# Head norms of an attention: the reciprocal root as exp(-ln/2) on ScalarE in place of a VectorE reciprocal and a ScalarE root

## The chip, the cores and the metric

The kernel runs as one program on one core of a Trainium2 chip. A core has five engines that run side by side, each through its own list of instructions in order: TensorE (PE, matrix products, with its weight loads shown as PEld), VectorE (DVE), ScalarE (ACT), GpSimd (POOL) and SyncE (SP, which here only issues DMAs). They wait for each other by semaphores. The metric is the time of one execution on the device, in microseconds (us). The kernel before took 3070.99 us in the median of three runs (3069.37 to 3074.17).

## What is computed

Two layers with a mixer and a feed-forward part each; the second layer's mixer is an attention with 16 heads of 64 numbers, whose queries and keys are normed per head before the scores:

```
def rms_norm(x, g):
    xf = x.astype(jnp.float32)
    y = xf * lax.rsqrt(jnp.mean(xf * xf, axis=-1, keepdims=True) + NORM_EPS)
    return (y * g.astype(jnp.float32)).astype(x.dtype)

def fox_mixer(h, in_w, f_b, q_norm_g, k_norm_g, out_w):
...
    q, k, v, f_logit, og = jnp.split(h @ in_w, [D, 2 * D, 3 * D, 3 * D + H], axis=-1)
    q = rms_norm(q.reshape(B, S, H, E), q_norm_g)
    k = rms_norm(k.reshape(B, S, H, E), k_norm_g)
...
        s = jnp.einsum('bhqe,bkhe->bhqk', qb, k).astype(jnp.float32) * scale
        s = s + cq[..., None] - cum[:, :, None, :]
        s = jnp.where(qpos[:, None] >= key_pos[None, :], s, -jnp.inf)
        p = jax.nn.softmax(s, axis=-1)
        return jnp.einsum('bhqk,bkhe->bqhe', p.astype(v.dtype), v)
```

The sequence has S = 512 tokens, the width is D = 1024, E = 64. The change concerns `lax.rsqrt(mean + NORM_EPS)` in the two head norms, and nothing else.

## The kernel before

The program runs the first layer (a gated recurrence, then a feed-forward part that picks experts), then the attention, then the second layer's feed-forward part. Matrix products keep single precision by splitting each operand into a high and a low part (`hi`, `lo`) and adding three products; the splits cost ScalarE a copy and VectorE a subtraction each (`split`, L252 and L253; for weights, L180 and L182).

The attention is `fox`. The heads are worked off in eight pairs, since two heads of 64 fill the 128 partitions. For each pair j:

- `prepare(j)` calls `heads_norm`. It projects the queries and the keys of the pair (`proj_t`, 24 matmuls each, L496 to L498, tile pacc of which there are two). ScalarE squares each projection (sq, L1348) and copies it with its gain (raw, L1350). Matmuls with a matrix of ones sum the squares over each head into one tile of 128x256 in PSUM (ssq, L1352), where the sums for queries and keys of both heads and both halves of the tokens stand in eight of its rows. Then comes the reciprocal root of that tile: VectorE scales and adds the epsilon (L1355) and takes the reciprocal (L1356), ScalarE takes the root (L1357). The tile is split (rh on ScalarE, rl on VectorE), spread over the partitions by matmuls (rsb, L1366 and L1367) and multiplied into raw (L1368). After this, ScalarE and VectorE make the operands qs, qx, ks, kx of the scores (L1395 to L1408).
- `attend(j)` takes the two heads in turn, and in each four blocks of 128 queries: scores (s, L1426 and L1427), mask (L1428), row maximum (nm, L1430), exponential (p, L1433, on ScalarE), its reciprocal sum and scaling (L1434, L1435, on VectorE), transposes on TensorE (tp, L1438), a split of these (pth and ptl, L252 and L253), and the products with the values (o, L1443 to L1445).

Pairs 0 and 1 are prepared first; after that pair j + 2 is prepared behind the attention of pair j, and behind the last two pairs the gates of the output (`gate`) are projected instead. So TensorE always has projection matmuls that depend on little beside the weights, and they stand between the matmuls of the attention, which wait for ScalarE and VectorE.

The order on each engine isn't that of the code: a scheduler lays it out when the program is built, by its own estimates of how long each instruction takes, except for instructions that are pinned to the order of the code (`keep_in_program_order`). From then on it is fixed. ScalarE needs a table of coefficients for its functions; the program's builder puts a load of another table (ACT_TABLE_LOAD) ahead of an instruction whose function isn't in the table that is loaded. [...]

Beside the attention, a few rows of the next stage's modulation are computed on VectorE (`during`, L215), and SP and POOL fetch weights.

Of the kernel before, what the change touches and what calls it, by code (L numbers as in the profile page):

```python
# [4 lines left out]
F32 = mybir.dt.float32  # L5
# [5 lines left out]
AF = mybir.ActivationFunctionType  # L11
OP = mybir.AluOpType
# [9 lines left out]
EPS = 1e-6  # L22
FH = 16
FE = 64
# [226 lines left out]
def split(g, hi, lo, raw, eng=None):  # L251
    g.nc.scalar.activation(hi, raw, AF.Copy)  # L252
    (eng or g.nc.vector).tensor_sub(lo, raw, hi)  # L253
# [235 lines left out]
def proj_t(g, psum, h, n=S, bank=None):  # L489

    nc = g.nc
    whi, wlo = g.stream.take()
    hhi, hlo = h
    ps = (psum.tile([128, S], F32, name="pacc", tag="acc") if bank is None else bank)[:, :n]
    for k in range(KD):
        nc.tensor.matmul(ps, whi[:, k, :], hhi[:, k, :n], start=(k == 0), stop=False)  # L496
        nc.tensor.matmul(ps, whi[:, k, :], hlo[:, k, :n], start=False, stop=False)  # L497
        nc.tensor.matmul(ps, wlo[:, k, :], hhi[:, k, :n], start=False, stop=(k == KD - 1))  # L498
    return ps
# [748 lines left out]
def fox(g, norm_fn, fb, qg, kg, during, grow_fn, after):  # L1248

    tc, nc = g.tc, g.nc  # L1250
    V, A, T = nc.vector, nc.scalar, nc.tensor
    cx = g.dram.tile([FH, 2, 4, S], F32R, name="cx")
    with pool(tc, name="foxy", bufs=1) as fy:
# [4 lines left out]
        with pool(tc, name="fox", bufs=1) as fp:  # L1258
# [28 lines left out]
            kgc = fp.tile([128, 1], F32, name="kgc")  # L1287
            nc.sync.dma_start(kgc, kg)
            V.tensor_scalar(qgc, qgc, FE ** -0.5, None, op0=OP.mult)
            fbc = fp.tile([FH, 1], F32, name="fbc")  # L1290
            nc.sync.dma_start(fbc, fb)
            sel = fp.tile([128, 128 + NU * 4 - 2], F32, name="sel")
# [5 lines left out]
            def chosen(i, u):  # L1298

                r = NU * 4 - 2 - u * 4 - i * 2  # L1300
                return sel[:, r:r + 128]
# [35 lines left out]
            with pool(tc, name="foxw", bufs=2) as fw, \  # L1337
                    pool(tc, name="fps", bufs=2, space=PSUM) as psum:

                def heads_norm(parts):  # L1340

                    n = S // NU
                    ss = psum.tile([128, n], F32, name="ssq", tag="n", bufs=1)
                    raw = []
                    for i, gc in enumerate(parts):
                        ps = proj_t(g, psum, h)
                        sq = fw.tile([128, S], F32, name="sq", tag="sq", bufs=1)
                        A.activation(sq, ps, AF.Square)  # L1348
                        r = fw.tile([128, S], F32, name="raw", tag=f"raw{i}")
                        A.activation(r, ps, AF.Copy, scale=gc)  # L1350
                        for u in range(NU):
                            T.matmul(ss, chosen(i, u), sq[:, u * n:(u + 1) * n], start=(i == 0 and u == 0),  # L1352
                                     stop=(i == 1 and u == NU - 1))
                        raw.append(r)
                    V.tensor_scalar(ss, ss, 1.0 / FE, EPS, op0=OP.mult, op1=OP.add)  # L1355
                    V.reciprocal(ss, ss)  # L1356
                    A.activation(ss, ss, AF.Sqrt)  # L1357
                    rh = fw.tile([128, n], F32R, name="rh", tag="rh", bufs=1)
                    rl = fw.tile([128, n], F32R, name="rl", tag="rl", bufs=1)
                    split(g, rh, rl, ss)  # L1360
                    out = []
                    for i, r in enumerate(raw):
                        b = psum.tile([128, S], F32, name="rsb", tag="n", bufs=1)
                        for u in range(NU):
                            us = slice(u * n, (u + 1) * n)
                            T.matmul(b[:, us], selT[:, i, u, :], rh, start=True, stop=False)  # L1366
                            T.matmul(b[:, us], selT[:, i, u, :], rl, start=False, stop=True)  # L1367
                        V.tensor_mul(r, r, b)  # L1368
                        out.append(r)
                    return out  # L1370
# [15 lines left out]
                def prepare(j):  # L1386
                    qn, kn = heads_norm((qgc, kgc))
                    stacks = []
                    for par in range(2):
                        own = slice(par * 64, par * 64 + 64)  # L1390
                        oth = slice(64 - par * 64, 128 - par * 64)
                        hd = j * 2 + par
                        qs = fw.tile([128, S], F32R, name="qs", tag="qs", bufs=4)
                        qx = fw.tile([68, S], F32R, name="qx", tag="qx", bufs=4)
                        A.activation(qs[own], qn[own], AF.Copy)  # L1395
                        V.tensor_sub(qs[oth], qn[own], qs[own])
                        A.activation(qx[0:64], qn[own], AF.Copy)
                        nc.gpsimd.dma_start(qx[64:68], cx[hd, 0])
                        stacks.append([qs, qx])
                    for par in range(2):  # L1400
                        own = slice(par * 64, par * 64 + 64)
                        oth = slice(64 - par * 64, 128 - par * 64)
                        hd = j * 2 + par
                        ks = fw.tile([128, S], F32R, name="ks", tag="ks", bufs=4)
                        kx = fw.tile([68, S], F32R, name="kx", tag="kx", bufs=4)
                        A.activation(ks[own], kn[own], AF.Copy)
                        A.activation(ks[oth], kn[own], AF.Copy)
                        V.tensor_sub(kx[0:64], kn[own], ks[own])  # L1408
                        nc.gpsimd.dma_start(kx[64:68], cx[hd, 1])
                        stacks[par] += [ks, kx]  # L1410
                    return stacks
# [58 lines left out]
def model(tc, *aps):  # L1470
# [4 lines left out]
    with ExitStack() as ctx:  # L1475
# [35 lines left out]
        def flat(n):  # L1511
# [7 lines left out]
             lambda p: mod("l0_ffn", p, gate, 4, ring=8), lambda p: mod("l1_mix", p, bufs=4, ring=8),  # L1519
             lambda p: mod("l1_ffn", p, first[:M1], 4, ring=8), 3, PUMPS[0])  # L1520
        fox(g, normed("l1_mix"), *arg("fox_", "fb", "qg", "kg"), lambda p: (mod("l1_ffn", p, first[M1:], 1),),
            grow("l1_mix"), lambda p: ())
        peer(g, normed("l1_ffn"), flat("l1_u"), flat("l1_v"), grow("l1_ffn"),
# [98 lines left out]
```

## Time and profile before

| what | us |
|---|---|
| median of three runs | 3070.99 |
| lowest, highest run | 3069.37, 3074.17 |
| the profiled execution | 3075.46 |
| span in its trace | 3073.7 |
| the stretch in which heads are normed and attended, from 1569 to 1789 us | 220 |

The profiled execution is one of its own, with its own time; the span is the part of it from the first to the last instruction, 1.8 us shorter. Times in the trace are counted from the start of the span. By stages the engines were busy as follows (one row for each stretch; busy us of each engine with the number of instructions, then the granted TensorE clock, the share of the DMA engines and GB/s):

```profile
520.00:1420.00 900.00, 894.90 (x4981) 803.93 (x4980) 788.94 (x1020) 399.09 (x544) 401.11 (x296) 1.00 0.95 360
1420.00:1569.00 149.00, 145.80 (x678) 122.03 (x676) 107.11 (x177) 62.73 (x102) 15.16 (x29) 1.00 0.48 169
1569.00:1789.00 220.00, 214.93 (x1107) 172.84 (x1106) 189.50 (x457) 175.32 (x365) 18.05 (x35) 1.00 0.21 71
1900.00:3073.00 1173.00, 1161.38 (x6429) 1050.54 (x6427) 980.61 (x1877) 513.25 (x690) 429.61 (x326) 1.00 0.81 297
```

The first number behind the stretch is its length, then PE, PEld, DVE, ACT, POOL. A line of a group reads: line of the code, engine, operation, output and inputs by the program's names, shapes, how often, busy time and mean duration in ns, and the idle time of that engine just before it with what ended that. A line of the waits reads: who waited for whom, us in total, times, longest. PEld waits are those of the weight loads, which run ahead of the matmuls.

### The profile page before, as it was taken

What the parts mean: (1) busy time and instruction counts of PE and PEld (TensorE: products, weight loads), DVE (VectorE), ACT (ScalarE), POOL (GpSimd) and SP (SyncE); (2) the same over time, 40 slices, a digit from 0 to 9 for tenths busy, and PEclk for the clock granted to TensorE, in tenths of its full rate; (3) what the DMA queues carried; (4) which work ended last, traced back from release to release, by engine and by line L of the source; (5) the groups of instructions that cost most, each with busy time, mean ns of one, the idle gap of its engine ahead of it and who ended that gap; (6) DMA issues with size and microseconds to landing.
All of it is one profiled execution on the core that took longest, in us unless ns stands there. A gap on an engine that the chain in (4) does not pass through costs nothing.

```text
span 3073.7 us, 44567 instructions
## 1 busy us (share of the span) xinstructions
PE 3021.1 (98%) x16196; PEld 2672.5 (87%) x16196; DVE 2567.1 (84%) x5272; ACT 1479.7 (48%) x2184; POOL 972.2 (32%) x842
## 2 busy tenths in 40 slices
PE   7999999999999999999999999999999999999999
PEld 5778899998888888888777778899998888888888
DVE  7866989878889888898679868799968888888787
ACT  6764247873333333333468843367853333333332
POOL 0001430006665145563011003400035544445451
PEclk9999999999999999999999999999999999999999
DMA  7543345779999999998332123346799999999995
GB/s 286 177 159 129 103 148 207 263 292 394 393 375 396 351 356 382 384 370 316 123 114 85 63 110 127 120 167 242 271 350 377 349 357 349 355 344 359 346 339 189
DMA packets 295470, 815.85 MB, mean 265 GB/s; under 512 B 24625, under 2 KB 147537, under 8 KB 266705
## 3 DMA queue, kind: packets, MB, share of 16 engines
q1 hardware_dynamic: 164304, 388.77, 35.3%
q0 software_dynamic: 89408, 321.43, 27.7%
q10 hardware_dynamic: 41536, 102.80, 8.7%
q8 instruction: 127, 2.08, 0.3%
q14 instruction: 95, 0.77, 0.1%
HBM read 731.89 MB, written 81.02 MB: 264 GB/s over the span
## 4 chain that ended last, share of the span: by engine, by line
PE 75%; DVE 13%; issue 5%; ACT 3%; DMA 3%; POOL 0%; DVEq 0%; SPq 0%; POOLq 0%; ACTq 0%
PE vacc L1159 31%; PE pacc L496 11%; PE pacc L498 11%; PE pacc L497 11%; PE gps L1002 3%; DMA at<-ascr 2%; DVE wlo L182 2%; DVE accg L1072 1%; PE oacc L539 1%; PE oacc L540 1%; PE oacc L538 1%; DVE ge L909 1%; DVE tk L834 1%; DVE idxs L833 1%; DVE idxs L836 1%
## 5 line engine op out<-in xcount | busy, mean ns | idle before, releaser
L180 ACT ACTIVATE whi<-wraw 128x1024 fp32r<-128x1024 f32 (+1 forms) x646 | 663.6, 1033 | 579.4 <-PE pacc L497 338.2
L496 PE MATMUL pacc<-hhi,whi 128*128 128x384 f32 (+1 forms) x2600 | 915.3, 352 | 0.0
L498 PE MATMUL pacc<-hhi,wlo 128*128 128x384 f32 (+1 forms) x2600 | 908.7, 350 | 6.1 <-DVE wlo L182 5.8
L497 PE MATMUL pacc<-hlo,whi 128*128 128x384 f32 (+1 forms) x2600 | 906.7, 349 | 0.0
L182 DVE TENSOR_TENSOR wlo<-wraw,whi 128x1024 fp32r<-128x1024 f32 (+2 forms) x580 | 699.2, 1210 | 184.5 <-ACT whi L180 183.3
L1159 PE MATMUL vacc<-whi,wl 128*128 128x512 f32 x1536 | 600.2, 391 | 0.0
L1159 PE MATMUL vacc<-wlo,wh 128*128 128x512 f32 x1536 | 599.9, 391 | 0.0
L1159 PE MATMUL vacc<-whi,wh 128*128 128x512 f32 x1536 | 597.6, 389 | 0.0
L498 PEld LDWEIGHTS pacc<-hhi,wlo 128*128 128x128 f32 x2600 | 488.7, 188 | 32.7 <-DVE wlo L182 9.8
L497 PEld LDWEIGHTS pacc<-hlo,whi 128*128 128x128 f32 x2600 | 489.2, 188 | 26.9
L496 PEld LDWEIGHTS pacc<-hhi,whi 128*128 128x128 f32 x2600 | 489.2, 188 | 26.4
L1149 ACT ACTIVATE wh<-at 128x384 fp32r<-128x384 f32 x256 | 133.9, 525 | 737.3 <-DVE at L1145 456.3
L1042 POOL DMA_INDIRECT rows<-in_l_u_dram,ei x256 | 383.3, 1497 | 280.5 <-DVE rows L1055 221.7
L1042 POOL DMA_INDIRECT rows<-in_l_v_dram,ei x256 | 369.0, 1441 | 322.0 <-DVE accg L1072 281.6
L1159 PEld LDWEIGHTS vacc<-whi,wl 128*128 128x128 f32 x1536 | 288.2, 188 | 60.3
L1159 PEld LDWEIGHTS vacc<-wlo,wh 128*128 128x128 f32 x1536 | 288.2, 188 | 57.5
L1159 PEld LDWEIGHTS vacc<-whi,wh 128*128 128x128 f32 x1536 | 288.4, 188 | 57.1
L1072 DVE SCALAR_TENSOR_TENSOR accg<-rows,act,accg 128x1024 f32<-128x1024 f32 x254 | 324.5, 1278 | 0.4
L1055 DVE SCALAR_TENSOR_TENSOR rows<-rows,hn 128x1024 f32<-128x1024 f32 x256 | 304.0, 1218 | 0.0
L1145 DVE TENSOR_TENSOR at<-at,gtile 128x384 f32<-128x384 f32 x256 | 140.7, 552 | 143.8 <-DMA at<-ascr 137.9
L1004 ACT ACTIVATE st<-gps 128x512 f32<-128x512 f32 x192 | 186.4, 1111 | 28.7 <-PE gps L1002 28.4
L182 POOL TENSOR_TENSOR wlo<-wraw,whi 128x1024 fp32r<-128x1024 f32 (+1 forms) x62 | 125.2, 2031 | 186.2 <-ACT whi L180 186.2
(317 smaller groups left out, 3409.9 us busy)
## 6 DMA issues: line engine op xcount, KB each, us to landing
wraw<-in_l_uT_dram SPq DMA_DIRECT2D x128, 1024.0 KB
wraw<-in_l_v_dram SPq DMA_DIRECT2D x128, 1024.0 KB
gscr<-st ACTq DMA_DIRECT2D x48, 1024.0 KB
gtile<-gscr SPq DMA_DIRECT2D x90, 512.0 KB
mw<-in_l_ffn_mw_dram POOLq DMA_DIRECT2D x48, 512.0 KB
ascr<-at ACTq DMA_DIRECT2D x112, 192.0 KB
at<-ascr ACTq DMA_DIRECT2D x112, 192.0 KB
mw<-in_l_mix_mw_dram POOLq DMA_DIRECT2D x32, 512.0 KB
```

The lines of the kernel that those rows point to most:

```text
L180: self.pin(nc.scalar.activation(hi, raw, AF.Copy))
L182: self.pin((nc.gpsimd if self.on_pool else nc.vector).tensor_sub(lo, raw, hi))
L496: nc.tensor.matmul(ps, whi[:, k, :], hhi[:, k, :n], start=(k == 0), stop=False)
L497: nc.tensor.matmul(ps, whi[:, k, :], hlo[:, k, :n], start=False, stop=False)
L498: nc.tensor.matmul(ps, wlo[:, k, :], hhi[:, k, :n], start=False, stop=(k == KD - 1))
L1004: A.activation(st[:, :, q * 4:q * 4 + 4].rearrange("p e t -> p t e"), gps, AF.Copy, scale=1.0 / GSCALE)
L1042: i = nc.gpsimd.indirect_dma_start(out=rows, out_offset=None, in_=src, in_offset=bass.IndirectOffsetOnAxis(ap=ei[:, j:j + 1], axis=0))
L1055: V.scalar_tensor_tensor(r, r, 1.0, hn, op0=OP.mult, op1=OP.mult, accum_out=act[:, j:j + 1]))
L1072: i = V.scalar_tensor_tensor(acc, r, w, acc, op0=OP.mult, op1=OP.add)
L1145: pin(V.tensor_tensor(at.rearrange("p (b t) -> p b t", t=16), at.rearrange("p (b t) -> p b t", t=16), gts[c // 8][:, :, c % 8, :], op=OP.m ...
L1149: pin(A.activation(wh, at, AF.Copy))
L1159: T.matmul(acc[t][d], x[:, ts], y[:, d, :], start=(i == 0 and x is wh and y is vh), stop=(i == PK - 1 and x is wl))
```

## The change

In `fox` a column epsc is filled with the epsilon, and in `heads_norm` three instructions become two: ln(ss/64 + epsilon), then exp(-1/2 of that), both on ScalarE and in place.

```
             nc.sync.dma_start(kgc, kg)
             V.tensor_scalar(qgc, qgc, FE ** -0.5, None, op0=OP.mult)
+            epsc = fp.tile([128, 1], F32, name="epsc")
+            V.memset(epsc, EPS)
             fbc = fp.tile([FH, 1], F32, name="fbc")
...
                         raw.append(r)
-                    V.tensor_scalar(ss, ss, 1.0 / FE, EPS, op0=OP.mult, op1=OP.add)
-                    V.reciprocal(ss, ss)
-                    A.activation(ss, ss, AF.Sqrt)
+                    A.activation(ss, ss, AF.Ln, scale=1.0 / FE, bias=epsc)
+                    A.activation(ss, ss, AF.Exp, scale=-0.5)
                     rh = fw.tile([128, n], F32R, name="rh", tag="rh", bufs=1)
```

Line numbers behind it shift, by two up to the norm and by one behind it. The scheduler lays out the stretch anew.

ScalarE at the seventh of the eight norms (ssq is the tile of the sums; p and l are the exponentials and their row sums, pth the split transposes). Before:

```order
L1350 ACTIVATE raw<-pacc,qgc 128x512
L1357 ACT_TABLE_LOAD
L1357 ACTIVATE ssq<-ssq 128x256
L252 ACTIVATE pth<-tp 128x3x128
L252 ACTIVATE pth<-tp 128x4x128
L1433 ACT_TABLE_LOAD
L1433 ACTIVATE p,l<-s,nm 128x128
L1433 ACTIVATE p,l<-s,nm 128x256
L252 ACTIVATE rh<-ssq 128x256
```

and in the changed program, at the same norm:

```order
L1434 ACTIVATE p,l<-s,nm 128x128
L1357 ACT_TABLE_LOAD
L1357 ACTIVATE ssq<-ssq,epsc 128x256
L1358 ACT_TABLE_LOAD
L1358 ACTIVATE ssq<-ssq 128x256
L252 ACTIVATE rh<-ssq 128x256
L1434 ACTIVATE p,l<-s,nm 128x256
L252 ACTIVATE vh<-vt 128x512
```

The two loads stand together now, with the logarithm between them, and rh follows at once; the load that stood ahead of the softmax's p is gone, since the exponential of the norm leaves its table in place. In six of the eight norms the four instructions stand unbroken as here; in the second a p (with its load), in the fourth a pth stands between logarithm and exponential. Counted over the eight norms there are 16 loads before (L1357 and L1433, eight each) and 16 now (L1357 eight, L1358 seven, L1434 one).

VectorE at the seventh norm (l the reciprocal sums of the softmax, nm its row maxima). Before:

```order
L1355 TENSOR_SCALAR ssq<-ssq 128x256
L1430 TENSOR_REDUCE nm<-s 128x1
L1356 RECIPROCAL ssq<-ssq 128x256
L1434 RECIPROCAL l<-l 128x1 x2
L1428 TENSOR_TENSOR s<-s,mask 128x128
L1435 TENSOR_SCALAR p<-p,l 128x384
L1435 TENSOR_SCALAR p<-p,l 128x512
```

and in the changed program, where it scales the same two blocks:

```order
L1435 RECIPROCAL l<-l 128x1 x2
L1429 TENSOR_TENSOR s<-s,mask 128x128
L1436 TENSOR_SCALAR p<-p,l 128x256
L1436 TENSOR_SCALAR p<-p,l 128x384
L1431 TENSOR_REDUCE nm<-s 128x1
L253 TENSOR_TENSOR ptl<-tp,pth 128x128
L253 TENSOR_TENSOR ptl<-tp,pth 128x2x128
L1435 RECIPROCAL l<-l 128x1
L1436 TENSOR_SCALAR p<-p,l 128x512
```

The scaling and the reciprocal of the norm have left the row; the scalings of the softmax blocks stand behind other work of the attention alone. The new column is filled on VectorE behind L1289:

```order
L509 TENSOR_TENSOR x_14395<-x_14395,gt 128x512 x2
L1289 TENSOR_SCALAR qgc<-qgc 128x1
L1291 MEMSET epsc 128x1
L1295 MEMSET sel 128x134
L1306 TENSOR_SCALAR mask<-ji 128x128
L1298 MEMSET sel 64x1 x2
L430 CAST hhi<-hk 128x384
```

There it stands ahead of the cast of hhi, the operand of the first matmul of the values.

## The prediction

> **What bounds the kernel now.** I read the profile from the outside in: first the page (span, busy shares, the chain that ended last), then the stretch in which the changed lines run, cut into windows, then the waits inside that stretch.
>
> ```profile
> span 3073.7 us, 44567 instructions
> PE 3021.1 (98%) x16196; PEld 2672.5 (87%) x16196; DVE 2567.1 (84%) x5272; ACT 1479.7 (48%) x2184; POOL 972.2 (32%) x842
> PE 75%; DVE 13%; issue 5%; ACT 3%; DMA 3%; POOL 0%; DVEq 0%; SPq 0%; POOLq 0%; ACTq 0%
> ```
>
> TensorE (PE) is busy 98% of the span and holds 75% of the chain. So over the whole program only the small share in which PE idles, or runs behind its weight loads (PEld), can be won. The changed lines run in one stretch alone; the rows of the reciprocal (with the first and last start of its eight instructions) and of the lines beside it say where:
>
> ```profile
> L1356 DVE RECIPROCAL ssq<-ssq x8: 1746/1752/1767, 1577.1 to 1732.9; 128x256 f32<-128x256 f32 x8
> L1355 DVE TENSOR_SCALAR ssq<-ssq x8: 404/422/433, 1576.6 to 1731.9; 128x256 f32<-128x256 f32 x8
> L1357 ACT ACT_TABLE_LOAD  x8: 1283/1283/1283, 1576.0 to 1734.6; - x8
> L1357 ACT ACTIVATE ssq<-ssq x8: 368/368/368, 1578.9 to 1735.9; 128x256 f32<-128x256 f32 x8
> ```
>
> Eight norms, one for each pair of heads, between 1576 and 1736 us; the attention that they feed ends near 1789 us. The busy times by window (each number is busy us, then the granted clock PEclk and the DMA) over that stretch:
>
> ```profile
> core 0: us, PE busy (x) PEld busy (x) DVE busy (x) ACT busy (x) POOL busy (x), PEclk, DMA share, GB/s
> 1560.00:1580.00 20.00, 20.00 (x89) 16.29 (x88) 8.38 (x12) 7.44 (x10) 3.15 (x6) 1.00 0.49 170
> 1580.00:1640.00 60.00, 57.51 (x294) 46.69 (x293) 52.69 (x121) 49.21 (x97) 6.36 (x12) 1.00 0.23 76
> 1640.00:1780.00 140.00, 137.93 (x725) 110.69 (x723) 126.88 (x322) 116.69 (x252) 11.47 (x22) 1.00 0.21 69
> 1780.00:1800.00 20.00, 18.66 (x90) 14.71 (x89) 12.57 (x22) 10.54 (x21) 2.10 (x4) 1.00 0.53 208
> ```
>
> Before 1580 us PE is full. From 1580 to 1800 us it idles 2.49 + 2.07 + 1.34 = 5.9 us. The last of these is mostly one wait at the end of the attention, which the change doesn't touch:
>
> ```profile
> L538 PE MATMUL oacc<-whi,yhi 128*128 128x512 f32 x1 | 0.5, 503 | 1.3 <-ACT yhi L252 1.3
> ```
>
> That leaves 5.9 - 1.3 = 4.6 us of visible idle time. One head pair in the steady part shows how near all three engines are to full:
>
> ```profile
> 1706.57:1730.43 23.86, 23.51 (x125) 19.12 (x125) 21.27 (x54) 21.10 (x46) 2.07 (x4) 1.00 0.15 45
> ```
>
> Of 23.86 us PE is busy 23.51, VectorE (DVE) 21.27, ScalarE (ACT) 21.10. PE binds, but neither of the others has much room. What PE and its weight loads waited for from 1580 to 1780 us (total us, times, longest):
>
> ```profile
> PE s L1426 <- ACT p L1433: 1.8, 3, 0.9
> PE ssq L1352 <- ACT sq L1348: 1.0, 2, 0.7
> PE o L1443 <- ACT pth L252: 1.0, 4, 0.3
> PE rsb L1366 <- DVE raw L1368: 0.2, 1, 0.2
> PEld s L1426 <- ACT p L1433: 7.9, 22, 1.3
> PEld o L1443 <- ACT pth L252: 4.8, 12, 0.7
> PEld tp L1438 <- DVE p L1435: 2.8, 6, 0.5
> ...
> PEld rsb L1366 <- DVE raw L1368: 1.2, 3, 0.6
> ...
> PEld rsb L1366 <- DVE rl L253: 0.3, 1, 0.3
> ```
>
> PE itself waits 1.8 + 1.0 + 1.0 = 3.8 us for ACT and 0.2 us for DVE. Its weight loads run ahead of it, so their waits (2.8 + 1.2 + 0.3 = 4.3 us for DVE) delay PE only in part. This is the heart of the case: **the change unloads DVE, and PE waits mostly for ACT**. A part of ACT's own lateness goes back to DVE, though, by the row maxima that the softmax needs:
>
> ```profile
> ACT p L1433 <- DVE nm L1430: 6.3, 7, 1.3
> ```
>
> **What the change removes.** Eight scalings and eight reciprocals leave DVE: 8 x (0.422 + 1.752) = 17.4 us, 2.17 us for each head pair, so DVE falls from 21.27 to about 19.1 of 23.86 us. None of it was a term of PE's path by itself: no row of PE's waits names L1355 or L1356. What it can give is that the DVE instructions queued behind a reciprocal, which blocks the queue for 1.75 us, come earlier. The ends are 0 (PE never saw it) and -4.3 us (every weight-load wait on DVE was a wait of PE and goes). I take **-2.8 us**, the row of tp behind p, since these transposes wait on the very scalings (L1435) that stand behind a reciprocal in DVE's order; the two rsb rows I leave, as they wait on other DVE work.
>
> **What it adds.** On ACT, the root becomes a logarithm and an exponential on the same 128x256 tile. Neither is in the trace on that shape, so they are estimated: the exponential, with an immediate scale as the root has, at the root's 0.368 us; the logarithm has a column as its bias, and what a column operand costs shows in two rows that differ by it, both 128x512 out of the same tile:
>
> ```profile
> L1350 ACT ACTIVATE raw<-pacc,qgc x8: 677/694/697, 1568.9 to 1710.6; 128x512 f32<-128x512 f32 x8
> L1348 ACT ACTIVATE sq<-pacc x16: 576/580/603, 1568.4 to 1726.4; 128x512 f32<-128x512 f32 x16
> ```
>
> 0.694 - 0.580 = 0.11 us, so the logarithm is some 0.48 us. ACT gains 8 x 0.48 = 3.8 us of work. The number of table loads stays: the root needed one and the softmax behind it another,
>
> ```profile
> L1433 ACT ACT_TABLE_LOAD x8 | 10.3, 1283 | 0.1
> ```
>
> that is 8 + 8, and the order of the changed program has 8 for the logarithm, 7 for the exponential of the norm and 1 for the softmax: 16 again. Only their place differs. ACT goes from 21.10 to about 21.6 us per head pair, still under PE's 23.5. The ends of what PE pays are 0 (covered by PE's projection matmuls) and +3.8 us (all of it seen). I take **+1.0 us**, the size of the row of o behind pth: a wait that comes about once a pair where ACT is already the late one, and which I let double.
>
> [...]
>
> **What it moves.** The order on PE, DVE and ACT is laid out anew from the second projection of the first norm to the end of the attention; behind that it is the same again, as is SP's queue. POOL swaps a few qx, kx and mw loads, whose waits are off PE's path (no PE row names them). A norm itself gets shorter: no DVE step stands between the sums and the root any more. That is worth nothing by itself, since the pair that it serves (but for the first two) is attended two pairs later. The new order can cost or gain; bounded by the visible idle time, -4.6 (all gone) to +4.6 us (doubled), I take 0. The added constant is one DVE memset of a column. It is small but not hidden: it stands in DVE's order where PE waits for DVE,
>
> ```profile
> 1496.35 0.15 DVE L1289 TENSOR_SCALAR qgc<-qgc 128x1 f32<-128x1 f32 x1
> 1496.48 0.17 DVE L1293 MEMSET sel<- 128x134 f32 x1
> ...
> 1497.31 0.50 PE L1275 MATMUL vacc<-whi,hhi 128*128 128x512 f32 x1 [1.07 <-DVE hhi L430]
> ```
>
> so it pushes that matmul back by the spacing of two such instructions, 1496.48 - 1496.35 = 0.13 us: **+0.1 us**.
>
> **Sum:** -2.8 + 1.0 + 0 + 0.1 = **-1.7 us**. The profiled execution took 3075.46 us, of which the span is 3073.7; it would be 3073.8 us. The median of the runs is 3070.99, 4.5 us lower than that execution, and a median is what I predict: 3070.99 - 1.7 = **3069.3 us**. That is within 0.2% (6.1 us), about what a measurement of this kernel can tell from no change.
>
> **Rivals.**
> *ACT's block (slower).* In the old order a load and a root stop ACT's other work for 1.28 + 0.37 = 1.65 us, and the second load often comes later. The chain can be read here (start, us, engine, line):
>
> ```profile
> 1644.22 1.28 ACT L1357 ACT_TABLE_LOAD   x1
> 1645.51 0.37 ACT L1357 ACTIVATE ssq<-ssq 128x256 f32<-128x256 f32 x1
> 1645.90 1.28 ACT L1433 ACT_TABLE_LOAD   x1
> 1647.19 0.37 ACT L1433 ACTIVATE p<-s,nm 128x128 f32<-128x128 f32 x1
> ```
>
> In the new order load, logarithm, load, exponential stand unbroken in six of eight norms: 1.28 + 0.48 + 1.28 + 0.37 = 3.41 us in which no p and no pth is made. It decides where PE has less than 3.41 us of projection work ahead of the next matmul that needs one of these. Consecutive projection matmuls start 0.23 us apart:
>
> ```profile
> 1579.67 0.39 PE L496 MATMUL pacc<-hhi,whi 128*128 128x512 f32 x1
> 1579.90 0.39 PE L497 MATMUL pacc<-hlo,whi 128*128 128x512 f32 x1
> ```
>
> so the point is 3.41 / 0.23 = 15 of them. Full price: six times what the block grew, 6 x (3.41 - 1.65) = 10.6 us, giving 3081.6 us (+0.34%). For it speaks that PE's waits are on ACT; against it, that the row at 1645.90 shows old blocks of 2.93 us already, so the real growth there is 0.48 us.
>
> *DVE was the hidden bound (faster).* All 4.6 us of idle time goes, and the 4.3 us of weight-load waits on DVE (less the 0.2 us counted in both): -8.7 us, 3062.3 us. For it: DVE's 89% in the steady pair, and ACT's 6.3 us behind DVE's maxima. Against it: ACT is as full.
>
> *One load serves logarithm and exponential.* Then ACT saves 8 x 1.283 = 10.3 us and adds 3.8, and PE's 3.8 us of waits for ACT would go with the 2.8 us of DVE's: -6.6 us, 3064.4 us. The order has the loads, so this is nearly excluded. That the change doesn't do what it says, DVE keeping its two instructions, is excluded by the order too: both groups are gone.
>
> **How the numbers follow.** Forecast 0.75 (its own range is the terms' ends, -4.3 - 4.6 + 0.1 = -8.8 to 3.8 + 4.6 + 0.1 = +8.5 us about the median, most of it within 5); ACT's block 0.13; hidden DVE bound 0.10; one load 0.02. So faster by over 0.2%: 0.10 + 0.02 = 0.12; within: 0.75; slower: 0.13. The range goes down to the DVE rival and up to the terms' upper end, 3070.99 + 8.5 = 3079.5: 3062.0 to 3079.5, leaving out most of ACT's block and thin tails.
>
> **What would show it.** Right: DVE near 19.1 us per head pair and 17 us less in all; 16 table loads of 1.283 us between 1570 and 1740; the logarithm at 0.44 to 0.52 us; the steady pair still 23 to 24 us long with PE at 98%; tp's waits on p smaller, o's and s's waits on ACT slightly larger. Wrong upward: PE waits on p or pth of over 1 us behind the loads of L1357 and L1358. Wrong downward: a pair under 23.3 us. A change outside 1570 to 1800 us of more than the memset's 0.1 us would refute the whole reading.

## The result, and the profile after

The changed kernel took 3097.71 us in the median (3095.57 to 3100.32), the kernel before 3072.95 us beside it: a ratio of 1.0086 (95% interval 1.0076 to 1.0096). It is slower by some 25 us, far above the range of the prediction. First the page of the changed kernel: the span, the busy time of each engine, the shares of the chain that ended last.

```profile
span 3095.1 us, 44562 instructions
PE 3026.1 (98%) x16196; PEld 2675.2 (86%) x16196; DVE 2557.7 (83%) x5257; ACT 1483.8 (48%) x2192; POOL 969.6 (31%) x842
PE 71%; DVE 16%; ACT 6%; DMA 4%; issue 3%; POOL 0%; SPq 0%; DVEq 0%; ACTq 0%; POOLq 0%
```

DVE did less (2557.7 for 2567.1 us; in the stretch of the norms 13 us less by the rows below, where the prediction has 17) and ACT barely more; yet PE's share of the chain fell from 75 to 71%, and DVE's and ACT's rose. The new instructions themselves are as predicted (line, operation, ns min/median/max, first and last start):

```profile
L1357 ACT ACT_TABLE_LOAD  x8: 1283/1283/1283, 1574.9 to 1752.0; - x8
L1357 ACT ACTIVATE ssq<-ssq,epsc x8: 448/448/448, 1576.2 to 1753.3; 128x256 f32<-128x256 f32 x8
L1358 ACT ACT_TABLE_LOAD  x7: 1283/1283/1283, 1576.7 to 1753.7; - x7
L1358 ACT ACTIVATE ssq<-ssq x8: 368/368/374, 1578.0 to 1755.0; 128x256 f32<-128x256 f32 x8
```

The logarithm took 0.448 us (predicted 0.48), the exponential 0.368, and 15 loads stand in the norms. The loss lies in the stretch of the norms alone. From the first matmul of ssq to the first of oacc it was 220.7 us before (1569.1 to 1789.8) and is 243.1 now (1567.9 to 1811.0); below, "the stage" means this, with starts read to 0.1 us. The busy times of the whole stage before and after, and of the longest window that the prediction shows of before (same columns):

```profile
1569.06:1789.83 220.77, 214.87 (x1108) 172.83 (x1107) 190.12 (x458) 176.07 (x367) 18.88 (x36) 1.00 0.21 71
1567.94:1811.02 243.08, 218.79 (x1108) 175.39 (x1107) 177.06 (x441) 179.98 (x375) 20.02 (x38) 0.99 0.21 72
1640.00:1780.00 140.00, 124.64 (x649) 99.77 (x648) 108.87 (x277) 109.60 (x233) 11.08 (x21) 0.99 0.17 53
```

In the stage PE stood idle for 5.9 us before (220.77 - 214.87) and for 24.3 us now, 18.4 us more. The other 3.9 us are longer busy time for the same 1108 matmuls, up to 3.4 us of it PE's clock (an estimate, last section). In the same 140 us PE was busy 137.93 us before and 124.64 now, and started 649 matmuls for 725. The three largest rows of what it waited for from 1569 to 1820 us:

```profile
PE s L1427 <- ACT p L1434: 10.6, 9, 2.8
PE rsb L1367 <- DVE rl L253: 5.5, 4, 1.8
PE o L1444 <- ACT pth L252: 2.2, 1, 2.2
```

The largest of these waits come one behind each norm, as three of the first row, the four of the second and the one of the third. The seventh norm before the change, without the rows between (start, us, engine, line):

```profile
1706.41 1.03 PE L1352 MATMUL ssq<-sq,sel 128*128 128x256 f32 x4
...
1711.32 1.28 ACT L1357 ACT_TABLE_LOAD   x1
...
1712.61 0.37 ACT L1357 ACTIVATE ssq<-ssq 128x256 f32<-128x256 f32 x1
...
1715.99 0.38 ACT L252 ACTIVATE rh<-ssq 128x256 fp32r<-128x256 f32 x1
...
1716.60 0.42 DVE L253 TENSOR_TENSOR rl<-ssq,rh 128x256 fp32r<-128x256 f32 x1
...
1718.00 0.28 PE L1366 MATMUL rsb<-rh,selT 128*128 128x256 f32 x1
```

and after it:

```profile
1723.88 0.59 PE L1354 MATMUL ssq<-sq,sel 128*128 128x256 f32 x2
...
1724.44 1.28 ACT L1357 ACT_TABLE_LOAD   x1
...
1725.73 0.45 ACT L1357 ACTIVATE ssq<-ssq,epsc 128x256 f32<-128x256 f32 x1
...
1726.20 1.28 ACT L1358 ACT_TABLE_LOAD   x1
...
1726.72 0.27 PE L1446 MATMUL o<-pth,vl 128*128 128x128 f32 x1
1727.49 0.37 ACT L1358 ACTIVATE ssq<-ssq 128x256 f32<-128x256 f32 x1
1727.89 0.38 ACT L252 ACTIVATE rh<-ssq 128x256 fp32r<-128x256 f32 x1
...
1728.31 0.42 DVE L253 TENSOR_TENSOR rl<-ssq,rh 128x256 fp32r<-128x256 f32 x1 [2.47 <-ACT rh L252]
...
1728.79 0.39 PE L1367 MATMUL rsb<-rh,selT 128*128 128x256 f32 x1 [1.79 <-DVE rl L253]
```

Before, PE had 10.6 us of other work between the sums (ssq, which end at 1707.44) and their spread (rsb), and rl, the last that rsb needs, was done 1 us ahead of it (1717.02). Now PE's order brings rsb 15 matmuls behind the sums, some 2.5 us (1724.47 to 1726.99), while load, logarithm, load, exponential, rh and rl take 4.3 us in one line (1724.44 to 1728.73): PE stands still for 1.79 us. Counted in the traces, PE's matmuls between the last of ssq and the first of rsb are, for the eight norms:

| | 1 | 2 | 3 | 4 | 5 | 6 | 7 | 8 |
|---|---|---|---|---|---|---|---|---|
| before | 24 | 29 | 42 | 98 | 54 | 56 | 56 | 56 |
| after | 15 | 15 | 14 | 12 | 11 | 24 | 15 | 10 |

The largest waits behind the eight norms are 0.33, 1.83, 1.84, 1.51, 1.98, 2.15, 1.79 and 2.78 us, 14.2 us together.

### The profile page after: what moved, and what is told of

Its sections match the earlier page's. It is cut to its first block, busy times and chain, and to the rows that moved or that the text cites. A ratio compares the mean times of both kernels' runs of the same rounds, so it can differ in the third digit from the quotient of the medians.

```text
span 3095.1 us, 44562 instructions
## 1 busy us (share of the span) xinstructions
PE 3026.1 (98%) x16196; PEld 2675.2 (86%) x16196; DVE 2557.7 (83%) x5257; ACT 1483.8 (48%) x2192; POOL 969.6 (31%) x842
## 4 chain that ended last, share of the span: by engine, by line
PE 71%; DVE 16%; ACT 6%; DMA 4%; issue 3%; POOL 0%; SPq 0%; DVEq 0%; ACTq 0%; POOLq 0%
PE vacc L1159 30%; PE pacc L496 10%; PE pacc L498 10%; PE pacc L497 10%; PE gps L1002 3%; DVE wlo L182 2%; DMA at<-ascr 2%; DVE accg L1072 1%; DVE ge L909 1%; DVE tk L834 1%; PE oacc L540 1%; PE oacc L539 1%; PE oacc L538 1%; DVE idxs L833 1%; ACT whi L180 1%
```

## The experiments

Three explanations stood at the start: the loads stop ACT just where PE needs it; the new order is bad by itself; or ACT's 0.82 us of functions are too much (the root took 0.37). Two tools separate them. An order can be held: dependencies that only order, without semaphores, chain each engine's instructions in the stretch after a recorded list. And the loads can go: with one table set asked for by name, none stood ahead of the logarithm, of the exponential or of the softmax's (e2: one load from 1566 to 1815 us, at a gate, for 16 in the changed kernel). All medians are of 4 to 12 runs (of the kernel before, 6 to 33), each ratio against the kernel before beside it; stage and idle time are of one profiled execution each; "idle" adds up PE's waits of 0.15 us and more in the trace, from the norms to the first oacc matmuls. Code is shown without the bookkeeping that names instructions for the list.

| | order | loads in the norms | stage us | idle us | median us | ratio (95%) |
|---|---|---|---|---|---|---|
| before | old | 16 | 220.7 | 5.3 | 3071 to 3073 | 1 |
| after | new | 16 | 243.1 | 24.2 | 3097.7 | 1.0086 (1.0076 to 1.0096) |
| e1 | old | 16 | 228.2 | 11.7 | 3079.0 | 1.0023 (1.0014 to 1.0032) |
| e2 | new | 0 | 226.0 | 10.9 | 3078.0 | 1.0021 (1.0012 to 1.0031) |
| e3 | own | 0 | 225.7 | 10.4 | 3078.3 | 1.0018 (1.0009 to 1.0027) |
| e4 | old | 2 | 224.0 | 8.0 | 3076.8 | 1.0017 (1.0008 to 1.0026) |
| e5 | old, one gate moved | 0 | 220.1 | 5.3 | 3071.4 | 1.0003 (0.9995 to 1.0012) |
| e6 | new | 8, before Ln | 231.3 | 15.0 | 3083.0 | 1.0038 (1.0025 to 1.0051) |
| e7 | new | 8, before Exp | 234.2 | 18.3 | 3088.1 | 1.0055 (1.0042 to 1.0068) |
| e8 | new | 16, old arithmetic | 258.1 | 28.5 | 3108.7 | 1.0119 (1.0104 to 1.0134) |
| e9 | as e5 | 0 | 219.9 | 5.4 | 3069.7 | 0.9998 (0.9989 to 1.0008) |
| e10 | old | 16, old places | 222.7 | 6.5 | 3074.0 | 1.0009 (1.0000 to 1.0018) |
| e11 | own, loads planned | 16 | 226.3 | 10.8 | 3078.5 | 1.0024 (1.0015 to 1.0034) |
| e12 | that of e11 | 0 | 224.3 | 10.3 | 3075.5 | 1.0013 (1.0004 to 1.0022) |

The two columns fit together: the stage less this idle time, and less half of the time in it at half clock (6.8 us in the changed kernel, 30.7 in e8, 3.4 in e4, one such stretch, an estimate from the matmul shown there; none is taken for the others), is 214 to 216.5 us in every row. So what the versions differ by is PE standing still or running slow, and not the amount of its work.

**e1, the change in the old order.** The recorded list is that of the kernel before, with Ln and Exp in the root's place:

```
+        replay(tc, g.named)
...
+def replay(tc, named):
...
+        for p, q in zip(seq, seq[1:]):
+            tc.add_manual_dep(q, p.name, dep, reason="order")
```

> The arithmetic of the change in the order of the kernel before: on PE, DVE, ACT and POOL each instruction of the attention is held in the place that it had there; logarithm and exponential stand where the root stood, DVE's two instructions are left out, the loads follow by themselves (16 as in both). Theory A (the two loads in series, with logarithm and exponential between and behind them, stop ACT for 3.4 us, and PE needs p, pth or rl in that time): the old order leaves more matmuls between the sums and rsb, so the loads hurt less but still hurt; 3075 to 3081 us, the eight blocks still seen on ACT. Theory B (the new order is bad by itself, whatever the loads): all is back, 3069 to 3074 us. Theory C (the 0.82 us of ACT work per norm is too much for a full ACT): little changes, 3090 us or more.

The stage was 228.2 us: of the 22.4 us lost, 14.9 went with the new order and 7.5 stayed.

**e2, the new order without the loads.** The list is that of the changed kernel, with

```
+                A.preload_act_table_set("natural_log_exp_and_others")
                 ready = [prepare(0)]
```

> The changed kernel in exactly its own order on every engine, but with the table set that holds logarithm and exponential both loaded once, ahead of the first norm: no load stands in any of the eight norms. Theory A: the eight waits of PE behind the loads (0.3 + 1.8 + 1.8 + 1.5 + 2.0 + 2.2 + 1.8 + 2.8 = 14.2 us) go, and with them the stretches of half clock that followed two of them (some 3.4 us); 3076 to 3083 us. Theory B: the order stays, so the time stays, 3093 to 3100 us. Theory C: ACT loses 15 x 1.28 us of loads, which is more than the change added; at or under the kernel before, 3065 to 3073 us.

No load stood in the norms, and the stage was 226.0 us: in one and the same order the loads cost 17.1 us, PE's clock included. But 5.3 us over the kernel before stayed, which no load explains.

**e3, one set, laid out anew.** The same line, without a held order.

> As the run before, but the scheduler lays out the order anew, without the loads. Theory A: faster than the kernel before, since ACT loses 20 us of loads and DVE 17 us of work: 3062 to 3071 us. Theory B: an order laid out anew is a draw; anything from 3065 to 3100 us. Theory C: 3062 to 3071 us.

Much as e2: 225.7 us.

**e4, the old order, one set.**

> Logarithm and exponential from one table set, in the order of the kernel before. Two loads are left in the stretch, around a gate's tanh ahead of the last norm, and one behind it. Theory A: a little faster than the kernel before, 3064 to 3071 us, as the waits of PE for p and pth that stand behind loads there go too. Theory B: like the kernel before, 3069 to 3074 us. Theory C: 3064 to 3071 us.

The median of 3076.8 us lies above all three theories. One new wait stood out, and the other waits were those of the kernel before:

```profile
1736.98 0.80 PE L1445 MATMUL o<-pth,vh 128*128 128x512 f32 x1 [2.65 <-ACT pth L253]
```

A gate's activation (sg) stood ahead of the last norm there. The builder put a load ahead of it and two into the norm, ahead of Ln (1732.62 us) and of Exp (1734.38 us), 1.28 us each. The matmul behind this wait took 0.80 us, one of the same shape behind the waits of e1 and e10 0.50 us (below), and the granted clock from 1566 to 1815 us was 0.99 for 1.00 in e5.

**e5, that gate moved** behind the last norm in ACT's list (names stand for the list's numbers):

```
-  sg
   Ln
   Exp
+  sg
```

> The change's arithmetic in the order of before, with one table set that serves Ln and Exp (as e4), and the one activation of a gate (sg) that stood ahead of the last norm's Ln, and so forced two loads around that norm, moved behind its Exp on ScalarE. Theory A (a load in the chain of the norm is what PE pays): the new wait of 2.65 us (o behind pth, 1736.98 us in e4) goes, with the 1.7 us of matmuls at half the clock behind it; stage 219 to 220.5 us, time 3071 to 3073 us, ratio 0.999 to 1.001. Theory C (the 0.82 us of ScalarE's two functions per norm are too much by themselves): the wait stays or comes again elsewhere; stage 223 to 224 us, ratio 1.0015.

The wait went; 220.1 us, the time of before. ACT has two functions instead of one here, but also no load in the norms; e10 below has all 16 loads and lies 2.0 us over before. So the third explanation doesn't account for the loss.

**e6 and e7, one load each.** The order and the set of e2, and in each norm one load put back, ahead of Ln (e6) or between the two (e7):

```
+                    A.preload_act_table_set("natural_log_exp_and_others")
                     A.activation(ss, ss, AF.Ln, scale=1.0 / FE, bias=epsc)
                     A.activation(ss, ss, AF.Exp, scale=-0.5)
```

> The order of the changed kernel and one table set (as e2), with one load of that set put back ahead of each of the eight logarithms and none ahead of the exponentials of the norm. Theory A (the block of ScalarE is what counts, load by load): a block of 1.28 + 0.45 + 0.37 = 2.1 us; the stage lies half way between e2's 226.0 and the changed kernel's 243.1 us, about 234.5, ratio 1.005. Theory A2 (PE has cover for one load, not for two): 226 to 229 us, ratio 1.002 to 1.003; the waits behind the norms below 0.6 us each. Theory B (the order alone): 226 us.

> As e6, but the one load stands ahead of each of the eight exponentials of the norm, in the middle of its chain, and none ahead of the logarithms. If only the length of ScalarE's block counts: the same as e6 within 1.5 us of stage. If the place in the norm's own chain counts (the load ahead of Ln can run while Ln still waits for the sums, the one ahead of Exp never can): e7 is slower than e6 by up to 8 x 1.28 = 10 us, stage 234 to 240 us against 226 to 230 us, with the waits of rsb behind rl back at 1 us and more.

Eight loads ahead of Ln cost 5.3 us (231.3 - 226.0), eight ahead of Exp 8.2. PE's waits show the difference, e6 first:

```profile
PE s L1429 <- ACT p L1436: 7.2, 9, 1.5
...
PE rsb L1369 <- DVE rl L254: 1.1, 2, 0.6
```

```profile
PE s L1429 <- ACT p L1436: 8.4, 9, 1.5
PE rsb L1369 <- DVE rl L254: 2.6, 3, 1.1
```

e6 lies between its two theories. e7's stage just reaches the range of its second theory, but 2.9 us above e6 is less than that theory asked: a load on ACT counts, and so does its place in the chain. Together the two make 13.5 of the 17.1 us, if they may be added; the rest is about the size of what PE's clock can have taken in the changed kernel (last section), whose granted clock from 1566 to 1815 us was 0.98, that of e6 and e7 0.99.

**e8, the old arithmetic in the new order.**

> The arithmetic of before (VectorE's scaling and reciprocal, ScalarE's root, with their loads) held in the order of the changed kernel on PE, ScalarE and GpSimd; on VectorE the two come back where the scheduler places them. Theory B (the new order is bad by itself, by the 5.3 us that e2 has over before): stage about 226 us or more, 220.7 + 5.3. Theory A with the order made for a short norm: the norm's chain is load 1.28, reciprocal 1.77, root 0.37 with ScalarE free in the middle, but rh follows at once in ScalarE's order and so waits; stage 235 to 245 us, waits of rsb and p behind the norm again 1 to 2 us each.

258.1 us, worse than any estimate: with 10 to 24 matmuls between ssq and rsb, the longer chain over DVE made PE wait up to 4.28 us at once, and its clock was halved for 30.7 us of the stage, which costs up to 15.4 us (an estimate, half of it). The new order is one for a short norm: in it, the old arithmetic costs 15.0 us more than the new one (258.1 - 243.1).

**e9, DVE's work put back** beside e5's arithmetic; rl is scratch here and is overwritten by the split later:

```
+                    V.tensor_scalar(rl, ss, 1.0 / FE, EPS, op0=OP.mult, op1=OP.add)
+                    V.reciprocal(rl, rl)
                     A.activation(ss, ss, AF.Ln, scale=1.0 / FE, bias=epsc)
```

> The kernel of e5 with VectorE's scaling and reciprocal of each norm put back at their places in the order of before, written to a scratch tile: the result doesn't need them, VectorE has the work of before, ScalarE that of the change without loads. It prices the relief of VectorE alone. If it is worth the 2.8 us that the prediction took: stage 220.1 + 2.8 = 222.9 us, and the row of tp behind p about 1 us or more. If PE pays only what its own wait on these transposes says: within 1 us of e5, 220 to 221 us, and ScalarE's 0.82 us per norm then cost nothing either (before: 220.7).

219.9 us: in the old order and without loads, the relief of DVE was worth nothing. The very row that carried its -2.8 us is unchanged, in e5 (without DVE's 17 us) and in e9 (with them):

```profile
PEld tp L1440 <- DVE p L1437: 3.0, 6, 0.6
```

```profile
PEld tp L1446 <- DVE p L1443: 3.0, 6, 0.6
```

**e10, the loads at their old places.** Compared with e1, the second load is moved from between Ln and Exp to the first exponential of the softmax behind; one more load stands ahead of the first norm:

```
+                    A.preload_act_table_set("natural_log_exp_and_others")
                     A.activation(ss, ss, AF.Ln, scale=1.0 / FE, bias=epsc)
                     A.activation(ss, ss, AF.Exp, scale=-0.5)
+                    A.preload_act_table_set("exp_and_others")
```

> The change's arithmetic in the order of before with all 16 loads of before at the very places that they had there: one ahead of the logarithm (which, with the exponential, takes the place of the root), one ahead of the first exponential of the softmax behind it. Nothing but the place of the second load differs from e1, where it stands between logarithm and exponential. Theory A' (the place of a load, not the number, is what PE pays): stage 220 to 222.5 us, ratio 0.9995 to 1.001. Rival (each load, or each us of ScalarE's work in this stage, costs about what it costs in e1, 8 us for 16): about 228 us, ratio 1.002 to 1.003.

222.7 us for 228.2, 0.2 above what the theory of the place expected and far from its rival. The seventh norm in e1 (ACT, then PE):

```profile
1715.66 1.28 ACT L1359 ACT_TABLE_LOAD   x1
1716.95 0.37 ACT L1359 ACTIVATE ssq<-ssq 128x256 f32<-128x256 f32 x1
1717.23 0.97 ACT L253 ACTIVATE pth<-tp 128x384 fp32r<-128x384 f32 x2
```

```profile
1718.26 0.50 PE L1445 MATMUL o<-pth,vh 128*128 128x512 f32 x1 [1.57 <-ACT pth L253]
```

and in e10:

```profile
1713.39 0.37 ACT L1360 ACTIVATE ssq<-ssq 128x256 f32<-128x256 f32 x1
1713.67 0.97 ACT L253 ACTIVATE pth<-tp 128x384 fp32r<-128x384 f32 x2
1714.67 1.28 ACT L1361 ACT_TABLE_LOAD   x1
```

```profile
1714.70 0.50 PE L1447 MATMUL o<-pth,vh 128*128 128x512 f32 x1 [0.29 <-ACT pth L253]
```

The load steps from ahead of pth to behind it, and PE's wait falls by 1.57 - 0.29 = 1.28 us: one load.

**e11, the loads in the plan.** In the changed kernel the builder inserted the loads behind the scheduler. Here they are instructions that the scheduler sees, tied in one row behind the sums; `last` is the last matmul of the sums:

```
+                    chain(tc, last, A.preload_act_table_set("natural_log"),
+                          A.activation(ss, ss, AF.Ln, scale=1.0 / FE, bias=epsc),
+                          A.preload_act_table_set("exp_and_others"),
+                          A.activation(ss, ss, AF.Exp, scale=-0.5))
```

> The changed kernel with its 16 loads written out as instructions of the program (one ahead of each Ln, one ahead of each Exp of the norm), so that the scheduler lays out the stretch with them in its plan; in the changed kernel the builder put them in behind the scheduler. Same work, same number of loads. Between the last matmul of the sums (ssq) and the first of the spread (rsb) PE's order now holds 17, 19, 38, 33, 31, 27, 28, 24 matmuls in the eight norms, against 15, 15, 14, 12, 11, 24, 15, 10 in the changed kernel and 24, 29, 42, 98, 54, 56, 56, 56 before. Theory (the layout was made for a norm without loads, and that is why they cost 17 us there): most of the waits of 1.5 to 2.8 us behind the norms go, stage 226 to 233 us, ratio 1.002 to 1.005. Rival (15 or 16 loads in series cost what they cost, wherever PE's matmuls stand): stage 240 to 245 us, ratio 1.008.

226.3 us for 243.1, with the same 16 loads. Of the waits behind the norms one is left in the row that made 5.5 us:

```profile
PE rsb L1369 <- DVE rl L253: 0.6, 1, 0.6
```

**e12, the order of e11 without loads.**

> The order of e11 held on every engine, with one table set for Ln and Exp and so none of the 16 loads. If the 5.9 us by which e2 (220.1 to 226.0 us) lies over e5 come from too few matmuls of PE between the sums and the spread: with 17 to 38 of them the stage is 219.5 to 222 us, time 3069 to 3073 us, as before or a little under it. If they come from something else in a new layout (the last gate's activation, the softmax placed closer behind the scores): 224 to 227 us, ratio 1.001 to 1.002.

224.3 us, so the gap between ssq and rsb isn't all of e2's 5.9 us over e5. No wait stands at a spread any more; one of 2.05 us stands behind the modulation rows (`during`; DVE had waited 2.22 us for their weights, mw, by DMA), and 2.0 us more than before at the last gate and the first oacc matmul (0.97 + 1.92 + 0.46, for 1.33). These last also stand in e2, e11 and, within 0.1 us, e3.

## Why the prediction was wrong

The 22.4 us of the stage divide, by runs that follow on one another, into: the new arithmetic with all loads at their old places +2.0 (e10 against before; DVE's relief, 0 by e5 against e9, is in it); the second load moved into the norm +5.5 (e1 against e10); the new order +14.9 (after against e1). These are stages of single executions, and the medians give the same steps within some 3 us; the first step alone isn't clear of noise (ratio 1.0000 to 1.0018). The split depends on the path: in the new order without loads the change cost 5.3 us (e2), and in the old order the change with its loads cost 7.5 us (e1). The other 9.6 us come only where both meet.

- **"-2.8 us", DVE.** Wrong. The transposes' weight loads wait as long with DVE's reciprocals as without; the row named who was late, not that it was late because of a reciprocal. The other end, 0, was right.
- **"+1.0 us", ACT's work.** The mechanism and nearly the size were right for loads that stay where they were: 2.0 us, inside 0 to 3.8. The step that failed is the sentence behind it, "Only their place differs". The place was 5.5 us even in the old order, as ACT's next pth stood behind the moved load.
- **"The new order can cost or gain; bounded by the visible idle time ... I take 0".** This is the step that failed most. Idle time bounds what an order can win, not what it can lose: the order cost 14.9 us with the loads in it (5.3 without), and PE's idle went from 5.3 to 24.2 us. It rested on "A norm itself gets shorter ... That is worth nothing by itself, since the pair that it serves ... is attended two pairs later". The pair is, but rsb isn't: the new order had moved it from 24 to 98 matmuls behind the sums to 10 to 24, and the prediction read the order of ACT and DVE without reading that of PE, the engine that waits.
- **"+0.1 us", the constant.** Too small to show: the first ssq matmul starts between 1565.3 and 1569.1 us in these executions, the changed ones and the others mixed.
- **The rival "ACT's block"** was right in kind (PE waits on p and pth of over 1 us behind the loads, as it said), with 10.6 us as full price. Its condition, fewer than 15 projection matmuls to cover the block, was met: in the last six norms PE has 2 to 9 between ssq and rsb. The argument against it, "the real growth there is 0.48 us", compared blocks of ACT but not what PE had to do beside them. And it left out rsb, the third that waits.
- **One load for both.** The rival was put as nearly excluded, since the order has the loads. They can go all the same: with one set asked for by name ahead of the first norm, none stood in the norms (e2). Left to itself, the builder put 15 there. But asking for the set brought no gain over before (e3: ratio 1.0018, in a layout of its own); why isn't shown in full, as said below.
- **"A change outside 1570 to 1800 us ... would refute the whole reading"**: none is clear of the spread. The first ssq matmul starts some 1 us earlier than before, inside the spread of 1565.3 to 1569.1 us. From the first oacc matmul to the end of the span it is 3073.7 - 1789.8 = 1283.9 us before and 3095.1 - 1811.0 = 1284.1 after; the other runs have 1280.5 to 1284.5.

Why the scheduler chose this order, e11 shows in the main: what it didn't see, it didn't cover. With the loads in its plan, PE's order has 17 to 38 matmuls between ssq and rsb, and 16.8 of the 22.4 us go; e3, laid out anew with no load planned in the norms, has 8 to 23 there. That e11 also ties the four instructions together wasn't tried apart. What stays open is why its layouts without the reciprocal end some 4 to 6 us over the old one even without loads (e2, e3, e12). The waits are named above; the choices behind them weren't tried. No version was measurably faster than the kernel before; e5 and e9 equal it.

## What to carry to other kernels

Where instructions are added behind the scheduler (table loads here), count them into each chain that it shortened: compare, on the engine that waits, how much work stands between producer and consumer with how long the chain takes with everything in it. The price of a load depended here on where it stood: at the seventh norm PE waited 1.57 us for pth with the load ahead of that copy (e1) and 0.29 us with the load behind it (e10), 1.28 us less, the length of a load. And the idle time of the bottleneck bounds what a new order can gain, never what it can cost.

## What the hardware showed beside it

PE's granted clock fell from 1.00 to 0.50 for stretches of 3.41 us (in e8 also of twice that). In the changed kernel they begin at 1594.74, 1673.25 and 1813.19 us, 78.51 and 139.94 us apart: 23 and 41 times 3.413 us, as on a fixed grid. In the first of them a projection matmul starts 0.42 us behind the one before (1595.04 to 1595.46), soon after it 0.23 us (1599.10 to 1599.33). Two of the three, each with the stretch ahead of it:

```profile
1591.33:1594.74 3.41, 1.69 (x8) 1.33 (x9) 1.48 (x6) 3.03 (x9) 0.00 (x0) 1.00 0.71 274
1594.74:1598.15 3.41, 3.41 (x16) 3.12 (x14) 2.29 (x8) 1.31 (x4) 1.54 (x3) 0.50 0.04 7
1669.84:1673.25 3.41, 1.43 (x7) 0.90 (x6) 1.28 (x4) 3.37 (x8) 0.00 (x0) 1.00 0.48 151
1673.25:1676.66 3.41, 3.41 (x16) 2.95 (x15) 2.63 (x10) 1.71 (x6) 0.00 (x0) 0.50 0.00 0
```

Ahead of each of the three PE was busy for at most 1.72 of 3.41 us; stretches of this stage with 1.90 us or more weren't followed by a halving, though one with 1.67 us (from 1751.76) wasn't either, so these counts give no border. The waits of 1.83 us (to 1593.06) and of 1.98 us (to 1672.69) lie, but for 0.1 us of the first, in one such stretch each, and a halving followed. Those of 2.15 us (1699.85 to 1702.00) and of 2.78 us (1753.42 to 1756.20) lie across two, with borders at 1700.56 and 1755.17 us, and none followed. By the clock of 0.50 a halving can cost up to 3.41 / 2 = 1.7 us, an estimate. Two lie within the stage of the changed kernel, up to 3.4 us, about what e6 and e7 leave of the loads' price (17.1 - 13.5 = 3.6 us); that their stages have none isn't shown.

No cost of a table load beyond its own 1.283 us shows in the seventh norm of the changed kernel: the next function started 1.29 us after the load's start (1724.44 to 1725.73, and 1726.20 to 1727.49).
